# Ordering a two-layer hybrid backbone kernel by the scheduler's timing simulator

## The chip, the cores and the metric

The kernel runs on one core of a Trainium2 chip. The metric is the device time of one execution in microseconds, taken as the median over runs; before the change it is 2683.18 us over 3 runs (2682.48 to 2686.78).

## What is computed

The reference is a backbone of two layers (DEPTH = 2) over 256 latent tokens with a prefix of 256 context tokens, width 1024. Each layer has a token mixer with three branches and a SwiGLU feed-forward network, and layer norms after both. In layer 0 latent and context tokens both go through; layer 1, the last, gives only the latent tokens.

```python
def mixer_sublayer(...):
    (hq_l, hff_l, hfb_l, hi_l, hg_l, aq_l, ak_l, av_l, mz_l, mx_l, mdt_l, gt_l) = jnp.split(h_lat @ w_in, IN_SPLITS, axis=-1)
    ...
    y = g_hg * (o_hg @ w_br_hg) + g_at * (o_at @ w_br_at) + g_mb * (o_mb @ w_br_mb)
    return y @ w_out
```

Branch `hg` is HGRN2, a gated linear recurrence in both directions with 8 heads; branch `at` is grouped-query attention with 8 query and 2 key heads; branch `mb` is the Mamba-2 state-space scan (SSD) in both directions, 32 heads in 4 groups. The input projection has 14912 columns, the feed-forward network 2816 hidden units. All data are float32.

## The kernel before

Activations lie with channels on the 128 partitions and tokens along the free axis: 512 columns (context, then latent) in layer 0, mostly 256 in layer 1. Every large product is made as three matmuls in a reduced float32 type, from a high and a low half of each factor (`mm3`): high by high, high by low, low by high.

**Weights.** The class `Weights` streams each weight in tiles of 128 by 1024. `_load` (L115) starts the transfer on SyncE's queue into one of 4 buffers (`wraw`); `_split` makes the high half on ScalarE (`wh`, L125) and the low half on VectorE (`wl`, L126), 3 buffers each. `take` keeps the loads 4 tiles and the splits 2 tiles ahead of the unit of matmuls that reads them. These matmuls write the PSUM tiles `g`, of which there are 3. All matmuls are recorded under L204, transposes under L208, ScalarE's operations under L190, most of VectorE's under L193, L196, L200 and L201.

**Order of the work.** The program is written as generators. `Weave` steps through two of them together: a main one with projections (the `g` matmuls), and a side one with a scan or an attention whose operations are small. So the order in which the instructions are written down already interleaves the two. Per layer the stages are: the state-space scan's four groups (SSD), then the HGRN2 heads, the gates, attention, the branch projections, the output projection, and the feed-forward network.

**The order on each engine** is not this written order. When the `TileContext` closes, a list scheduler plays the program on a model of the chip. Whenever the model has an engine free, the scheduler gives it, of the instructions whose inputs are there, the one that comes first in the written order; a tile's buffer is given out in the same way. The resulting order per engine is then fixed in the program: on the chip each engine goes through its queue in that order, and an instruction that waits holds back those behind it. `issue_after` (at the transposes of `ssd_tok` and the activations of `silus`) adds edges that pin some instructions behind others.

**The SSD stage**, to which the prediction's steps go: `ssd_dt` computes decays and writes them to the DRAM tile `sd`. For each head, `ssd_scan` then loads two broadcasts of it on GpSimd's queue (L810 and L831 of the code below), builds the decay matrix and multiplies:

```python
for i in range(2):
    h = 8 * g + 2 * pr + i
    ab = self.b(name="ab")
    nc.gpsimd.dma_start(out=ab.rearrange("p (d t) -> p d t", d=2),
                        in_=bass.AP(sd.tensor, sd.offset + h * ts, [[0, P], [32 * ts, 2], [1, T]]))
    D, M = self.b(name="D"), self.b(name="M")
    ...
    e = self.a(name="ce")
    ...
yp = self.ps("y")
```

From `ab`, VectorE makes `D` and ScalarE parts of `M` (an exponential); ScalarE takes the exponential of `D`, VectorE adds parts of it into `M` and multiplies `M` by `cb` (L193). Then the matmuls `y<-M,xt` and `y<-ce,state` are made for the two heads in turn, which lie in two halves of the array's columns. `ab`, `D` and `M` come from a pool of 10 buffers (`n_b`), four of which hold `xt`, `cb` and `state` of the group. GpSimd's queue also carries other transfers: `sd` (L663, L666), the gates that layer 1 writes out early (`gd<-gate`, L1104), `ym`, `ys` and their reloads.

The line that is changed opens the `TileContext`; it is in `kernel`:

## Time and profile before

| | |
|---|---|
| median of 3 runs | 2683.18 us |
| the profiled execution's own time | 2682.9 us |
| its span, first to last instruction | 2681.0 us |
| mean granted TensorE clock | 0.991 of full |
| TensorE matmuls (PE) busy | 2597.5 us, 97%, 18660 matmuls |
| weight loads (PEld) busy | 2139.5 us, 80% |
| VectorE (DVE) busy | 1782.2 us, 66% |
| ScalarE (ACT) busy | 1233.2 us, 46% |
| GpSimd (POOL) busy | 193.0 us, 7% |
| DMA | 374.41 MB, mean 140 GB/s |

The profile is of one execution. Its own time is 1.9 us more than its span and 0.3 us under the median. A matmul's record overlaps the next one's, so that busy time of TensorE is time in which at least one is under way. "Idle before" an instruction is the time in which its engine had nothing, with what ended it after the arrow. SP is SyncE; a "q" after an engine marks what its sequencer issues, DMAs for instance. Names stand as out<-in.

### The profile page before, as it was taken

What the parts mean: (1) busy time and instruction counts of PE and PEld (TensorE: products, weight loads), DVE (VectorE), ACT (ScalarE), POOL (GpSimd) and SP (SyncE); (2) the same over time, 40 slices, a digit from 0 to 9 for tenths busy, and PEclk for the clock granted to TensorE, in tenths of its full rate; (3) what the DMA queues carried; (4) which work ended last, traced back from release to release, by engine and by line L of the source; (5) the groups of instructions that cost most, each with busy time, mean ns of one, the idle gap of its engine ahead of it and who ended that gap; (6) DMA issues with size and microseconds to landing.
All of it is one profiled execution on the core that took longest, in us unless ns stands there. A gap on an engine that the chain in (4) does not pass through costs nothing. (4 is left out here: it accounts for less than half of the span.)

```text
span 2681.0 us, 46307 instructions
## 1 busy us (share of the span) xinstructions
PE 2597.5 (97%) x18660; PEld 2139.5 (80%) x18660; DVE 1782.2 (66%) x3708; ACT 1233.2 (46%) x2030; POOL 193.0 (7%) x320
## 2 busy tenths in 40 slices
PE   7999989999999999999999999899999999999999
PEld 4767667788888897777888878677878898888998
DVE  5887776756565575457533358887877777857555
ACT  3655554632333324545432226565654334465543
POOL 0111010000000001010000000111110011111000
PEclk9999999999999999999999999899999999999999
DMA  7566555544444444352333323455763353446553
GB/s 248 147 178 178 147 163 157 150 120 116 118 142 134 123 138 154 94 194 70 102 95 102 95 79 99 132 161 161 222 185 108 98 144 109 140 122 201 166 183 109
DMA packets 298952, 374.41 MB, mean 140 GB/s; under 512 B 16433, under 2 KB 251985, under 8 KB 298737
## 3 DMA queue, kind: packets, MB, share of 16 engines
q1 hardware_dynamic: 271568, 284.21, 35.2%
q0 software_dynamic: 25728, 84.61, 11.1%
q8 instruction: 147, 2.41, 0.4%
q10 hardware_dynamic: 1440, 2.62, 0.3%
q14 instruction: 69, 0.56, 0.1%
HBM read 355.27 MB, written 16.12 MB: 139 GB/s over the span
## 5 line engine op out<-in xcount | busy, mean ns | idle before, releaser
L126 DVE TENSOR_TENSOR wl<-wraw,wh 128x1024 fp32r<-128x1024 f32 (+1 forms) x450 | 544.0, 1211 | 417.1 <-ACT wh L125 408.6
L125 ACT ACTIVATE wh<-wraw 128x1024 fp32r<-128x1024 f32 (+1 forms) x450 | 470.9, 1048 | 699.1 <-PE g L204 509.9
L204 PE MATMUL g<-hh,wh 128*128 128x512 f32 (+2 forms) x2032 | 731.8, 362 | 4.8 <-ACT hh L190 2.2
L204 PE MATMUL g<-hh,wl 128*128 128x512 f32 (+2 forms) x2032 | 723.0, 357 | 5.3 <-DVE wl L126 5.3
L204 PE MATMUL g<-hl,wh 128*128 128x512 f32 (+2 forms) x2032 | 724.6, 357 | 0.0
L204 PEld LDWEIGHTS g<-hh,wh 128*128 128x128 f32 (+1 forms) x2032 | 386.5, 191 | 75.9 <-issue 15.5
L204 PEld LDWEIGHTS g<-hh,wl 128*128 128x128 f32 (+1 forms) x2032 | 386.8, 191 | 68.7 <-issue 9.5
L204 PEld LDWEIGHTS g<-hl,wh 128*128 128x128 f32 (+1 forms) x2032 | 387.4, 191 | 61.8 <-issue 12.9
L204 PE MATMUL g<-oh,wh 128*128 128x512 f32 (+1 forms) x864 | 300.9, 350 | 2.4 <-DVE gl L193 1.3
L204 PE MATMUL g<-ol,wh 128*128 128x512 f32 (+1 forms) x864 | 295.3, 342 | 0.2 <-DVE ol L196 0.2
L204 PE MATMUL g<-oh,wl 128*128 128x512 f32 (+1 forms) x864 | 292.8, 340 | 0.5 <-DVE wl L126 0.5
L204 PE MATMUL g<-wh,hh 128*128 128x256 f32 x768 | 220.7, 287 | 0.0
L204 PE MATMUL g<-wh,hl 128*128 128x256 f32 x768 | 219.2, 285 | 0.0
L204 PE MATMUL g<-wl,hh 128*128 128x256 f32 x768 | 218.1, 284 | 0.0
L204 PEld LDWEIGHTS g<-oh,wh 128*128 128x128 f32 x864 | 163.7, 190 | 29.6 <-issue 7.9
L204 PEld LDWEIGHTS g<-ol,wh 128*128 128x128 f32 x864 | 164.3, 190 | 22.7 <-issue 6.3
L204 PEld LDWEIGHTS g<-oh,wl 128*128 128x128 f32 x864 | 164.0, 190 | 20.2 <-issue 2.7
L204 PEld LDWEIGHTS g<-wh,hh 128*128 128x128 f32 x768 | 147.1, 192 | 3.1 <-issue 2.6
L204 PEld LDWEIGHTS g<-wh,hl 128*128 128x128 f32 x768 | 147.2, 192 | 2.2 <-issue 1.9
L204 PEld LDWEIGHTS g<-wl,hh 128*128 128x128 f32 x768 | 147.2, 192 | 0.5 <-issue 0.4
L196 DVE SCALAR_TENSOR_TENSOR u<-craw,vec,u 128x508 f32<-128x508 f32 (+3 forms) x192 | 130.6, 721 | 8.6 <-ACT u L190 7.6
L196 DVE SCALAR_TENSOR_TENSOR D<-ab,tk,neg 128x128 f32<-128x128 f32 x384 | 110.2, 346 | 22.3 <-DMA ab<-sd 22.1
(303 smaller groups left out, 3577.7 us busy)
## 6 DMA issues: line engine op xcount, KB each, us to landing
wraw<-in_w_in SPq DMA_DIRECT2D x216, 512.0 KB, 4.1
wraw<-in_w_mod SPq DMA_DIRECT2D x96, 512.0 KB, 4.1
wraw<-in_w_ffn_in SPq DMA_DIRECT2D x88, 512.0 KB, 3.5
ab<-sd POOLq DMA_DIRECT2D x64, 512.0 KB, 6.8
wraw<-in_w_ffn_out SPq DMA_DIRECT2D x40, 512.0 KB, 3.4
ce<-sd POOLq DMA_DIRECT2D x64, 256.0 KB, 7.6
wraw<-in_w_br_mb SPq DMA_DIRECT2D x32, 512.0 KB, 3.4
wraw<-in_w_in SPq DMA_DIRECT2D x34, 256.0 KB, 3.6
```

The costliest lines, as they stand in the source:

```text
L125: self.nc.scalar.activation(hi[:, 0:n], t[:, 0:n], AF.Copy)
L126: self.nc.vector.tensor_tensor(out=lo[:, 0:n], in0=t[:, 0:n], in1=hi[:, 0:n], op=ALU.subtract)
L196: return self.nc.vector.scalar_tensor_tensor(out=out, in0=a, scalar=s, in1=b, op0=op0, op1=op1)
L204: return self.nc.tensor.matmul(out, l, r, start=start, stop=stop)
```

## The change

The `TileContext` is made with `schedule_with_timeline_sim=True`. The list scheduler then plays the program on the library's timeline simulator, in which queues and DMA transfers take time, in place of the plainer model. No line that computes is touched: the same instructions with the same sizes are scheduled, in an order that can differ on every engine and every DMA queue, and with buffers given out in another order.

```diff
-    with tile.TileContext(nc) as tc:
+    with tile.TileContext(nc, schedule_with_timeline_sim=True) as tc:
         with ExitStack() as ctx:
             Net(tc, io, ctx).run(out)
```

## Rows read from the trace of the kernel before

**Rows 1.** The page, part 1: span, and busy time of TensorE's matmuls.

```profile
span 2681.0 us, 46307 instructions
...
PE 2597.5 (97%) x18660; PEld 2139.5 (80%) x18660; DVE 1782.2 (66%) x3708; ACT 1233.2 (46%) x2030; POOL 193.0 (7%) x320
```

**Rows 2.** Busy time by stretch: us; busy (count) per engine; clock; DMA share; GB/s.

```profile
0.00:36.10 36.10, 17.29 (x256) 9.56 (x256) 10.04 (x33) 7.93 (x12) 3.01 (x9) 1.00 0.92 324
...
1340.00:1541.00 201.00, 201.00 (x889) 166.48 (x888) 72.66 (x79) 57.19 (x70) 0.00 (x0) 1.00 0.32 97
...
1676.00:2010.00 334.00, 307.06 (x1878) 247.69 (x1877) 266.93 (x528) 202.41 (x359) 52.12 (x76) 0.96 0.60 173
```

**Rows 3.** Waits of TensorE: engine, line, releaser, us in total, times, longest.

```profile
PE y L204 <- DVE M L193: 25.1, 13, 6.5
...
PE g L204 <- DVE wl L126: 5.8, 5, 2.3
```

**Rows 4.** Busy time by stretch: those in which the granted clock is half.

```profile
389.20:396.00 6.80, 3.83 (x9) 2.52 (x10) 6.01 (x14) 3.17 (x6) 0.00 (x0) 0.50 0.26 91
...
1727.20:1737.50 10.30, 7.48 (x29) 5.32 (x31) 5.81 (x13) 3.20 (x8) 2.14 (x3) 0.50 0.56 158
1812.60:1816.00 3.40, 3.40 (x14) 2.71 (x13) 3.23 (x6) 2.16 (x4) 2.13 (x3) 0.50 0.46 134
1979.80:1983.20 3.40, 3.40 (x16) 2.07 (x13) 1.15 (x4) 1.12 (x2) 0.71 (x1) 0.50 0.68 209
...
sum 47.80, PE 40.33 PEld 28.93 DVE 35.09 ACT 28.04 POOL 7.30; mean PE 5.04 PEld 3.62 DVE 4.39 ACT 3.50 POOL 0.91
```

**Rows 5.** Waits of all engines: two on landings, one on TensorE's release.

```profile
ACT wh L125 <- PE g L204: 509.9, 244, 7.5
...
ACT M L190 <- DMA ab<-sd: 51.3, 24, 5.6
...
DVE D L196 <- DMA ab<-sd: 22.1, 14, 4.9
```

**Rows 6.** Instructions in order of time, 380 to 393 us: start, length, engine, line.

```profile
380.30 0.71 POOL L810 DMA_DIRECT2D ab<-sd  x1 [11.07 <-PE g L204]
...
382.77 1.06 ACT L190 ACTIVATE D<-D 128x1024 f32<-128x1024 f32 x1 [1.47 <-DVE D L196]
...
383.25 1.22 DVE L126 TENSOR_TENSOR wl<-wraw,wh 128x1024 fp32r<-128x1024 f32 x1
...
389.41 0.61 DVE L196 SCALAR_TENSOR_TENSOR D<-ab,tk,neg 128x128 f32<-128x128 f32 x2 [4.95 <-DMA ab<-sd]
389.47 1.28 ACT L190 ACTIVATE M<-ab,tk 128x128 f32<-128x128 f32 x4 [5.64 <-DMA ab<-sd]
...
392.17 0.66 PE L204 MATMUL y<-M,xt 128*64 128x256 f32 x1 [6.50 <-DVE M L193]
```

**Rows 7.** Instructions in order of time, GpSimd's queue, 1677 to 1740 us.

```profile
1686.99 0.72 POOL L810 DMA_DIRECT2D ab<-sd  x1
1715.29 0.59 POOL L1104 DMA_DIRECT2D gd<-gate  x1 [27.57 <-ACT gate L190]
1719.64 0.56 POOL L1104 DMA_DIRECT2D gd<-gate  x1 [3.77 <-ACT gate L190]
...
1720.90 1.43 POOL L810 DMA_DIRECT2D ab<-sd  x2
```

**Rows 8.** The page, part 6: one group of DMA issues, us to landing.

```profile
ab<-sd POOLq DMA_DIRECT2D x64, 512.0 KB, 6.8
```

**Rows 9.** Groups by line, ScalarE: weight splits and table loads; busy us, mean ns.

```profile
L125 ACT ACTIVATE wh<-wraw 128x1024 fp32r<-128x1024 f32 (+1 forms) x450 | 470.9, 1048 | 699.1 <-PE g L204 509.9 <-issue 120.5 <-DMA wraw<-in_w_in 27.4
L190 ACT ACT_TABLE_LOAD x51 | 65.4, 1283 | 3.5 <-DVE s L196 1.9 <-PEq L1572 0.7
```

**Rows 10.** The chain that ended last: start, length, what.

```profile
1746.67 1.91 PE y L204 x14
...
2336.46 1.73 PE PV L204 x8
```

## The prediction

> **What bounds the kernel now.** The first view is the busy time of the engines: TensorE's matmuls cover 2597.5 of 2681.0 us, so it is without any work for 83.5 us [rows 1]. No other engine is above 66%. The next view is busy time by stretch. From 1340 to 1541 us TensorE is busy for all of 201.00 us: there the order of the instructions can give nothing. The first 36.1 us have 17.29 us of matmuls under a DMA share of 0.92 and 324 GB/s: weights of the modulation are awaited. The state-space scan of layer 1, from 1676 to 2010 us, has 307.06 of 334.00 us, so 26.9 us are idle, and its mean clock is 0.96 [rows 2]. Third come TensorE's own waits. The largest is that of the scan's `y` matmuls for `M` from VectorE, 25.1 us in 13 places [rows 3]. Fourth, the stretches at half the granted clock (1.2 in place of 2.4 GHz), 47.8 us in eight pieces; each begins behind idle time of TensorE, and a matmul there takes twice its time, so that they lose up to 23.9 us more [rows 4].
>
> How much room is that in all? The rows say 83.5 us idle plus 23.9 us of clock, 107 us or 4%, of which the start's 18.8 us (36.10 - 17.29) is a matter of transfers. The Trainium skill (Perfetto Trace Analysis, Identifying the Most-Contended Engine) holds matmul busy time for a poor measure and takes the busy share of the weight loads: at 80% that would leave 541 us, several times as much. Here the measurement decides: in the stretch without a gap the weight loads fill 166.48 of 201.00 us, 83%, so that 80% is nearly full [rows 1, 2].
>
> **What the change can move.** The same instructions run in another order. Rows show where the present order suits the transfers badly. At 380.30 us the load of `ab` is issued, and it is used at 389.41 us. VectorE's next instruction in the queue, a `D` that reads it, waits 4.95 us, and ScalarE's, an `M`, 5.64 us. Behind them in both in-order queues stand the next weight splits; TensorE ends its last `g` and waits 6.50 us at the `y` that needs this `M` [rows 6]. The median from issue to landing is 6.8 us, over 64 loads [rows 8]. In total ScalarE waits 51.3 us and VectorE 22.1 us for such landings at the head of their queues [rows 5]. A scheduler that gives a transfer time sees that the data are not there and puts the splits, and with them `g` matmuls, first. That is the mechanism I forecast.
>
> **The sum**, against the profiled execution's 2682.9 us (the median of the runs is 0.3 us above it):
>
> 1. Waits of `y` for `M`: 25.1 us [rows 3]. At best all go, at worst none. I take half, -12.5 us: the landing is hidden behind other work, but the `g` matmuls that can be drawn forward are few (three weight buffers, three PSUM tiles), and a late `ab` still delays `y`. What is late next is the buffer of `ab`, which comes free only when a head's work is done.
> 2. The clock behind these waits: the pieces at 389, 1727, 1812 and 1979 us last 6.8 + 10.3 + 3.4 + 3.4 = 23.9 us and lose up to half, 12.0 us [rows 4]. Half of that goes with the waits, -6.0 us; bounds 0 and -12.0.
> 3. GpSimd's queue: after the `ab` at 1686.99 us it waits 27.57 and 3.77 us for two gates to write out, and only then issues the next two `ab`, at 1720.90 us [rows 7]. Moved ahead, these loads would end the hunger for work there. The `y` waits are counted above; what is added are waits of `g` for `wl`, 5.8 us in five places [rows 3], of which I take 2.5. Bounds 0 and -5.8.
> 4. The start. All its loads must land in any order, and they take 0.92 of the DMA time of 36.1 us [rows 2]; a better order can gain 0.08 x 36.1 = 2.9 us, a worse one as much. I take 0.
> 5. SyncE's weight loads and the splits behind them: cost nothing, since ScalarE waits 509.9 us in 244 places for TensorE to free `wh` [rows 5]; the splits are early. If that cover went in one place, a split of 1.05 us would be on the path [rows 9].
> 6. Table loads of ScalarE: 51 of 1.283 us [rows 9]. Another mix of activations needs more or fewer, and one in front of a split that TensorE awaits is on the path. Bounds: ten fewer or ten more on the path, 12.8 us either way. I take three more, +3.8 us, because the scan's exponentials will stand among other work more often.
> 7. Order on TensorE. `y` matmuls of two heads share the array: 14 records in 1.91 us, 136 ns each, where undivided ones of the same width take 216 ns (8 in 1.73 us) [rows 10]. If `g` were put among them, 640 records would lose at most 80 ns each, 51 us. I take 0: they become ready together, and next to each other in the written order they stay together.
>
> Sum: 2682.9 - 12.5 - 6.0 - 2.5 + 3.8 = 2665.7 us, and with the median's 0.3 us 2666 us, 0.64% faster. With every wait of `y`, its clock and term 3 gone and no new table load it is 2683.2 - 25.1 - 12.0 = 2646 us, less up to 5.8; I set the low end at 2644.
>
> The Trainium skill (DMA: Bandwidth & Descriptors, Anatomy of one DMA) fits a GpSimd DMA as 2.0 us plus its bytes over 436 GB/s; an estimate by it for 512 KB is 3.2 us. The trace disagrees, with 6.8 us in the median [rows 8]. If the simulator reckons as that fit does, it speaks against the change: the order would hide only half of each landing, terms 1 and 2 would halve, and the time would be 2675 us.
>
> **The rivals.**
>
> *Nothing to be measured* (2683 us, within 5.4 us; 0.2% is about what a measurement of this kernel can tell from no change). For it: 83.5 us of idle time in 2681, and long stretches with none [rows 1, 2]; the order also goes by the written order, which is kept, so that engines swap only neighbours. What is moved off VectorE's and ScalarE's heads may have cost TensorE nothing: they wait 73.4 us for landings [rows 5], and TensorE only 25.1 us for `M`. That the order comes out as it was belongs here. Against it: 46307 instructions, and hundreds of choices that hang on times. Chance 0.21.
>
> *Slower, by GpSimd's queue.* It is in order and carries the loads of `ab` and `ce` together with writes of gates, which wait for a projection. Where a write gets in front of a head's load, the scan starves: that is what happens at 1715 us, and around it TensorE loses the 2.6 us of a `y` wait and about as much of a `wl` wait (term 3's 2.5) and half of the 10.3 us at half clock: 10.3 us in all [rows 4, 7]. With transfers that take time, a load has to wait longer in the model for its buffer, while the write's data are there when TensorE says so; so writes can get in front more often. Layer 1 has four groups with a gate chunk each; if it happens in two more, the time is 2683.2 + 20.6 = 2704 us. It decides from the point at which one more write stands in front than now without any `y` wait won. For it speaks that it is there once already; against it, that a simulator which knows the landing can also issue loads early. Chance 0.29, in which I put other new waits of the kind, table loads (term 6) and divided `y` groups (term 7) as well.
>
> **How the numbers follow.** Forecast, with its mechanism at any size over 0.2%: 0.50, its own range 2644 to 2677. No change: 0.21. Slower: 0.29. So faster 0.50, same 0.21, slower 0.29. The predicted time is that of the likeliest case, 2666 us. The range runs from 2644 to 2704 us: the low end is the whole of terms 1 to 3, the high end two more starved groups; beyond these I leave 0.05 below and 0.15 above (a starved group in all four, or divided `y` groups).
>
> **What would show it.** Right: in the changed kernel's trace ScalarE's `M` and VectorE's `D` wait well under 73.4 us for `ab`, `y` waits for `M` around 12 us, the half-clock pieces of the scans are fewer, and no `gd` write with a long wait stands between two `ab` loads of a group. Wrong: the landing waits are gone while TensorE's busy time and idle time stay (the rival without change); or idle time moves to other waits of `g` and `y`, with new pieces at half clock; or the table loads rise well over 51. The prediction also fails if the gain comes from the first 36 us, or from stretches that have no gap now.

## The result, and the profile after

The change makes the kernel slower: 2828.4 us (2826.0 to 2831.0, 4 runs) against 2685.0 us (2682.5 to 2687.5, 4 runs) of the kernel before on the same chip, a ratio of 1.0538 with a 95% interval of 1.0523 to 1.0554. The forecast was 2666 us, its range ended at 2704 us.

Of the experiments below, `list_pe2`, `list_all4`, `pe2_pool_plain` and `second_layer_pe2` were run 4 times and `first_layer_pe2` 10 times, the others once; runs of the kernel before lie between 2677.0 and 2690.1 us over all chips used.

First the page of the changed kernel: span and busy time.

```profile
span 2829.1 us, 46316 instructions
...
PE 2659.8 (94%) x18660; PEld 2166.4 (77%) x18660; DVE 1778.6 (63%) x3708; ACT 1226.6 (43%) x2023; POOL 192.8 (7%) x320
```

Against [rows 1] TensorE's idle time goes from 83.5 to 2829.1 - 2659.8 = 169.3 us, +85.8 us, and its busy time grows by 62.3 us over the same 18660 matmuls. VectorE, ScalarE and GpSimd work as long as before to within 7 us. So the other engines do no more work than before; TensorE stands bare twice as long, and its matmuls take longer.

A part of that is the clock. These are stretches of the changed kernel with half the granted clock, 24 in all without the end of the program: length, busy time of TensorE, its weight loads, VectorE, ScalarE, GpSimd, then clock, DMA share and GB/s.

```profile
1052.60:1059.40 6.80, 5.70 (x13) 3.16 (x14) 3.02 (x12) 2.50 (x6) 0.00 (x0) 0.50 0.25 77
...
1772.80:1789.80 17.00, 5.31 (x23) 4.18 (x22) 11.97 (x21) 5.16 (x10) 3.04 (x5) 0.50 0.41 102
...
2612.40:2626.10 13.70, 6.74 (x27) 5.87 (x27) 11.29 (x34) 8.69 (x19) 0.00 (x0) 0.50 0.16 50
...
sum 146.90, PE 105.01 PEld 79.97 DVE 109.50 ACT 64.21 POOL 19.37; mean PE 4.38 PEld 3.33 DVE 4.56 ACT 2.68 POOL 0.81
```

Before, there were eight such pieces with 47.8 us [rows 4]. What the slower clock lengthens is busy time: TensorE is busy in these stretches for 105.01 us, in those of before for 40.33 us, and half of the difference, at most 32.3 us, goes to the clock. With the 85.8 us of idle time that is 118 of the 148.1 us by which the span grew. The other 30 us are busy time too, and were followed only in part: the records of `mod` cover 82.2 us in place of 70.0, those of `y` (`M,xt` and `ce,state`) 129.6 us in place of 117.8, slower clock and overlap with other records included. Why stays open.

Where does it happen? Both kernels make the same 450 weight splits on VectorE (L126), and the starts of the 130th, 170th and so on cut both into comparable stages. Six stages of the kernel before, in the columns above: the first layer's scan (splits 0 to 60, counted from 0 in the order run), its HGRN2 heads (60 to 130), its attention (130 to 170), its output and feed-forward work (170 to 220), the boundary with the second layer's scan (220 to 300), the second layer's attention (340 to 390).

```profile
36.10:505.20 469.10, 453.33 (x2580) 330.52 (x2581) 369.89 (x716) 261.17 (x431) 47.05 (x67) 0.99 0.57 162
505.20:1010.50 505.30, 501.46 (x5146) 427.50 (x5146) 311.77 (x702) 169.92 (x242) 14.67 (x27) 1.00 0.43 127
1010.50:1312.50 302.00, 301.80 (x1596) 235.86 (x1595) 175.76 (x393) 149.23 (x265) 25.81 (x48) 1.00 0.40 128
1312.50:1584.00 271.50, 271.50 (x1199) 224.90 (x1198) 107.74 (x126) 75.57 (x92) 0.00 (x0) 1.00 0.31 94
1584.00:2039.20 455.20, 427.85 (x2628) 345.07 (x2627) 357.65 (x721) 271.95 (x490) 56.47 (x84) 0.97 0.53 152
...
2235.50:2490.50 255.00, 243.23 (x1963) 215.17 (x1962) 190.05 (x513) 136.31 (x246) 38.92 (x72) 0.97 0.47 146
```

And the same stages of the changed kernel:

```profile
35.60:535.50 499.90, 476.59 (x2615) 339.19 (x2614) 369.13 (x715) 264.29 (x433) 46.97 (x67) 0.97 0.54 155
535.50:1036.40 500.90, 500.12 (x5100) 427.25 (x5099) 306.52 (x687) 166.54 (x237) 14.63 (x27) 1.00 0.42 125
1036.40:1375.20 338.80, 319.10 (x1607) 243.77 (x1607) 179.09 (x411) 149.45 (x266) 26.11 (x48) 0.97 0.36 114
1375.20:1646.80 271.60, 271.60 (x1199) 224.87 (x1199) 107.77 (x127) 75.57 (x92) 0.00 (x0) 1.00 0.31 94
1646.80:2141.30 494.50, 441.21 (x2611) 349.23 (x2610) 356.84 (x720) 268.72 (x488) 56.45 (x84) 0.94 0.49 140
...
2342.80:2633.50 290.70, 249.37 (x1954) 219.43 (x1952) 193.80 (x518) 132.74 (x243) 38.58 (x72) 0.94 0.41 128
```

The feed-forward stage is equal to 0.1 us. The first attention loses 36.8 us, and it had not a microsecond of idle time before (301.80 of 302.00). The two attentions and the second scan lose 36.8 + 39.3 + 35.7 = 111.8 us, the first layer's scan another 30.8 (499.9 against 469.1 us). These are stages in which a chain of small operations runs beside the projections. The HGRN2 heads have such a chain too, and their stage is 4.4 us shorter; but the stages are cut at weight splits, and a piece of that chain has slid behind the cut (`oT` at 1045 us, below). The attention's chain of scores and transposes (`S`, `p`, `PT`, `PV`) contains no transfer.

TensorE's waits in the changed kernel (releaser, us in total, times, longest):

```profile
PE y L204 <- DVE M L193: 15.8, 7, 4.6
PE spread L204 <- DVE diag L193: 15.5, 5, 4.7
PE oT L208 <- DVE sq L196: 10.4, 5, 3.9
PE g L204 <- DVE hl L193: 9.3, 3, 3.6
PE dtT L208 <- DVE dy L193: 8.9, 1, 8.9
PE PT L208 <- DVE s L196: 7.2, 3, 3.3
...
PE g L204 <- DVE wl L126: 6.3, 4, 3.2
```

The wait that the forecast wanted gone, `y` for `M`, did shrink, from 25.1 us [rows 3] to 15.8. In its place stand many small ones, most of them at a matmul of a chain of small operations, the rest at projections that need its results (`hl`) or a split (`wl`). From the waits of the other engines:

```profile
ACT wh L125 <- PE g L204: 576.1, 270, 6.3
...
ACT M L190 <- DMA ab<-sd: 74.3, 25, 6.1
...
ACT oh L190 <- PE oT L208: 49.8, 14, 8.2
...
DVE D L196 <- DMA ab<-sd: 38.6, 20, 4.3
...
DVE ce L193 <- DMA ce<-sd: 9.9, 8, 2.1
```

and of the kernel before, for the second load of each head:

```profile
DVE ce L193 <- DMA ce<-sd: 23.5, 17, 3.6
```

The waits for landings of `ab` at the head of the two queues, 73.4 us before [rows 5], are now 112.9 us. With those for `ce` the sum goes from 96.9 to 122.8 us. A scheduler that knows of transfers has made them more, not fewer.

One place shows the pattern: instructions in order of time in the changed kernel's first attention (start, length, engine, line, what; in brackets the idle time before).

```profile
1041.11 1.13 DVE L196 SCALAR_TENSOR_TENSOR sq<-o,s,g 128x128 f32<-128x128 f32 x4
...
1044.77 0.39 PE L204 MATMUL g<-oh,wl 128*128 128x512 f32 x1
1045.00 0.27 PE L208 MATMUL oT<-ident,sq 128*128 128x128 f32 x1
...
1046.07 0.69 ACT L190 ACTIVATE oh<-oT,vec 128x512 fp32r<-128x512 f32 x1 [8.16 <-PE oT L208]
...
1049.37 1.06 ACT L125 ACTIVATE wh<-wraw 128x1024 fp32r<-128x1024 f32 x1 [2.12 <-PE g L204]
1050.44 1.28 ACT L190 ACT_TABLE_LOAD   x1
1051.74 0.56 ACT L190 ACTIVATE p<-S,s 128x256 f32<-128x256 f32 x1
...
1053.32 0.45 PE L208 MATMUL PT<-ident,p 128*128 128x128 f32 x1 [3.31 <-DVE s L196]
```

`sq` belongs to the last HGRN2 head. All four of its pieces are written by 1042.24 us, but TensorE's queue holds twelve more `g` ahead of the first `oT`, which starts at 1045.00, 2.8 us later. ScalarE stood idle for 8.16 us before `oh`. Then a weight split and a table load stand ahead of `p`, and between the last `g` and `PT` TensorE's queue holds no other matmul: TensorE is bare for 3.31 us, and the clock has gone to half at 1052.6 us, the first piece above. The projections were spent early, in front of the chain, and are missing when the chain is all there is.

### The profile page after: what moved, and what is told of

It reads as the page before. It is cut to its first block, busy times and chain, and to the rows that moved or that the text cites. A ratio compares the mean times of both kernels' runs of the same rounds, so it can differ in the third digit from the quotient of the medians.

```text
span 2829.1 us, 46316 instructions
## 1 busy us (share of the span) xinstructions
PE 2659.8 (94%) x18660; PEld 2166.4 (77%) x18660; DVE 1778.6 (63%) x3708; ACT 1226.6 (43%) x2023; POOL 192.8 (7%) x320
## 3 DMA queue, kind: packets, MB, share of 16 engines
q0 software_dynamic: 25728, 84.61, 10.4%
## 5 line engine op out<-in xcount | busy, mean ns | idle before, releaser
L126 DVE TENSOR_TENSOR wl<-wraw,wh 128x1024 fp32r<-128x1024 f32 (+1 forms) x450 | 544.5, 1210 | 500.5 <-ACT wh L125 489.7
L125 ACT ACTIVATE wh<-wraw 128x1024 fp32r<-128x1024 f32 (+1 forms) x450 | 471.5, 1049 | 768.4 <-PE g L204 576.1
L204 PEld LDWEIGHTS g<-hl,wh 128*128 128x128 f32 (+1 forms) x2032 | 390.5, 192 | 69.5 <-issue 10.4
L196 DVE SCALAR_TENSOR_TENSOR D<-ab,tk,neg 128x128 f32<-128x128 f32 x384 | 107.1, 344 | 39.3 <-DMA ab<-sd 38.6
```

Of the source, the lines that this page charges most:

```text
L125: self.nc.scalar.activation(hi[:, 0:n], t[:, 0:n], AF.Copy)
L126: self.nc.vector.tensor_tensor(out=lo[:, 0:n], in0=t[:, 0:n], in1=hi[:, 0:n], op=ALU.subtract)
L196: return self.nc.vector.scalar_tensor_tensor(out=out, in0=a, scalar=s, in1=b, op0=op0, op1=op1)
L204: return self.nc.tensor.matmul(out, l, r, start=start, stop=stop)
```

## The experiments

The kernels below are built twice in one program where orders are held: first with one model, to read its orders, then with the other, with an ordering edge (no semaphore) from each instruction of a held engine to the one ahead of it in the order read.

```diff
-    with tile.TileContext(nc) as tc:
-        with ExitStack() as ctx:
-            Net(tc, io, ctx).run(out)
...
+        with tile.TileContext(nc, schedule_with_timeline_sim=timeline) as tc:
+            with ExitStack() as ctx:
+                Net(tc, io, ctx).run(out)
+            pin(tc, nc, pins)
...
+        first, _ = build(PIN_FROM, {})
+        pins = orders(first)
...
+    nc, arrays = build(TIMELINE, pins)
```

**Is it the order at all?** The timing simulator, all five engines held to the plain model's orders.

> Scheduled on the timing simulator, but with the order of every engine and queue tied to that of the kernel before; only the giving out of buffers is left to the simulator. If the order makes the 143 us, as every theory here says: 2685 us, within 5. If the buffers given out matter: over 2700 us.

2679.4 us, with 2683.1 us of the kernel before on that chip. The loss is in the orders of the engines. Buffers given out differently cost nothing here: in this kernel, as built, 1033 of 4294 tiles lie at another address than before. SyncE's order is no part of it, since its instructions come in the same order in the kernel before, in the change and with every length of list below.

**Which engine's order?** Three mixtures: TensorE's order alone from the plain model, TensorE's order alone from the simulator, and VectorE's and ScalarE's from the plain model.

> Timing simulator, with TensorE's order alone tied to that of the kernel before. Theory T (TensorE's order does it: its g matmuls stand too far ahead of the scan's and attention's own matmuls, whose chain is then late and left bare): near before, 2685 to 2715 us. Theory V (the order of VectorE and ScalarE, splits against scan work): still over 2800 us. Theory P (GpSimd's queue, my rival): still over 2800 us.

> Plain model, with TensorE's order alone tied to that of the changed kernel; the other engines are ordered around it. Theory T: 2790 to 2830 us. Theories V and P: near before, under 2715 us.

> Timing simulator, with the orders of ScalarE and VectorE tied to those of the kernel before, TensorE free. Theory T: still slow, over 2780 us. Theory V: near before, 2685 to 2715 us. Theory P: over 2800 us.

They measured 2798.9, 2903.9 and 2896.3 us: 4.3, 8.2 and 7.9% over before, the last two worse than the change itself. None of the theories T, V and P meets all three: T wanted 2685 to 2715 us from the first, V and P under 2715 us from the second. Putting back TensorE's order alone, or VectorE's and ScalarE's, does not undo the loss, and the simulator's order on TensorE alone costs more than all of its orders together; the orders of one model fit each other. In the last two mixtures the splits come late. TensorE with the simulator's order above the plain model's splits:

```profile
PE g L204 <- DVE wl L126: 39.7, 8, 11.8
```

and the simulator's TensorE above the plain model's VectorE and ScalarE:

```profile
PE g L204 <- DVE wl L126: 41.7, 37, 3.7
...
PE g L204 <- ACT wh L125: 17.7, 12, 3.6
```

Before, that wait was 5.8 us [rows 3]. Mixing orders cannot separate the cause, and a new theory was needed. The simulator keeps, for each engine, a list of instructions that are handed over and not finished; the library's table gives it 35 places for TensorE and 12 for the others. Theory Q: an instruction gets its place in the order when it enters that list, many matmuls before it runs, when the side chain's next matmul isn't ready yet. The scheduler then fills the list with the ready `g` matmuls, and the chain's matmul stands behind them.

**How long a list?** The change itself, with the table altered only while the order is made:

```diff
+QDEPTH = {'PE': 2}
...
+    t = hw_specs.get_hw_spec("TRN2").ENG_ISSUE_QUEUE_DEPTH
+    kept = dict(t)
+    for e in t:
+        n = str(e).split(".")[-1]
+        if n in d:
+            t[e] = d[n]
...
+    table, kept = depths(QDEPTH)
...
+    nc, arrays = build(TIMELINE, pins)
+    table.update(kept)
```

> The edit: the timing simulator sets the orders as in the change, but while it does so, the list of instructions that it lets stand handed over and unfinished on TensorE is cut from 35 to 2 (the other engines keep 12). Theory Q (the scheduler has to choose a matmul when the simulator's list takes it, some 35 matmuls before it runs, so a matmul of the scan or of attention that becomes ready later stands behind that many of the projections): most of the loss goes, 2660 to 2710 us, TensorE idle near before's 83.5 us instead of 169.3. Theory L (the landings and durations in the simulator give the bad order, however long the list is): 2800 to 2850 us as in the change. Theory O (the lists of VectorE and ScalarE, 12 each, are what is too long): 2780 to 2840 us.

> The edit: as the change, with the simulator's lists of VectorE, ScalarE, GpSimd and SyncE cut from 12 to 2 and TensorE's left at 35. Theory Q (TensorE's list): 2800 to 2840 us, no more than 1% from the change. Theory O (the other engines' lists): 2660 to 2720 us. Theory L (landings, durations): 2800 to 2850 us.

> The edit: as the change, with the simulator's lists of all engines cut to 4 instructions. Theory Q: 2650 to 2710 us; if the simulator's landings are worth anything once the lists are short, this is below before, at 2655 to 2680. Theory O: 2650 to 2710 too. Theory L: 2800 to 2850 us.

> The edit: as the change, with TensorE's list in the simulator cut from 35 to 16 (the other engines keep 12). Theory Q: a loss that grows with the list, so between the run with 2 and the change, 2700 to 2770 us. Theories O and L: 2800 to 2850 us.

> The edit: as the change, with TensorE's list in the simulator lengthened from 35 to 70 (the others keep 12). Theory Q: the loss grows with the list, 2900 to 3000 us, with still more idle time of TensorE ahead of the matmuls of the scan and of attention. Rival S (35 is already long enough that nothing more is committed early, because the buffers of the weights end the run-ahead): 2810 to 2850 us.

The table gives the result by length of TensorE's list, with the length of three stages between the same weight splits, the mean granted clock, and the lead of the projections in the first attention. That lead is counted in the order on TensorE: for each matmul of the chain (`qT`, `S`, `PT`, `PV`, as far as they are among the first 11000 instructions written) the number of `g` matmuls ahead of it, less the number written ahead of it, and the mean of these.

| kernel | us | clock | first attention, us | second scan, us | second attention, us | lead of `g` |
|---|---|---|---|---|---|---|
| before (plain model) | 2684 | 0.991 | 302.0 | 455.2 | 255.0 | 18 |
| list of 2 | 2705.1 | 0.989 | 306.8 | 466.1 | 266.2 | 22 |
| list of 16 | 2736.1 | 0.984 | 314.5 | 476.5 | 282.8 | 40 |
| list of 35 (the change) | 2828.4 | 0.973 | 338.8 | 494.5 | 290.7 | 54 |
| list of 70 | 2943.7 | 0.958 | 353.0 | 507.3 | 314.1 | 59 |

With a list of 2 the ratio to before is 1.0073 (1.0052 to 1.0093): 123.3 of the 143.4 us that the change lost hang on one number in a table, and the loss grows with that number as theory Q expected. Rival S, that 35 is long enough already, falls with the list of 70. TensorE's idle time is then 2699.2 - 2594.6 = 104.6 us, not quite the 83.5 us of before. With all lists at 4 the ratio is 1.0076 (1.0057 to 1.0096); that short lists would bring the time below before did not come true. With TensorE's list at 35 and the others at 2, 2818.3 us: theory O falls. That the list's length decides, and that the lead in the first attention grows with it, is shown. That a matmul's place is settled when it enters the list is argued from this, and the mean lead doesn't measure the loss everywhere. Counted in the same way for the second layer's attention it is already 57 before, then 56, 60, 64 and 66 down the table, while that stage loses 11.2, 27.8, 35.7 and 59.1 us. With a list of 2, the waits are these, TensorE's first:

```profile
PE y L204 <- DVE M L193: 12.6, 14, 2.1
...
PE PT L208 <- DVE p L200: 4.7, 4, 1.6
PE oT L208 <- DVE sq L196: 4.4, 2, 3.8
...
PE spread L204 <- DVE diag L193: 1.4, 1, 1.4
```

```profile
ACT M L190 <- DMA ab<-sd: 73.3, 30, 6.4
...
DVE D L196 <- DMA ab<-sd: 31.1, 20, 3.7
...
ACT oh L190 <- PE oT L208: 23.5, 11, 4.5
```

The waits of `oT` and `spread` are less than half of the change's 10.4 and 15.5 us, and ScalarE waits 23.5 us for `oT` in place of 49.8. The landing waits of `ab`, however, are still 104.4 us, while 123 us of the time are gone: they were not what the change lost most by.

**Are the landings what is left?** The list of 2, and a start of GpSimd's transfers that is 3 us later in the simulator, so that consumers of `ab` are placed later.

```diff
+START = {'Pool': 3000}
...
+    t = hw_specs.get_hw_spec("TRN2").DGE_DMA_DELAY
+    old = dict(t)
...
+        for e in t:
+            t[e] += d.get(str(e).split(".")[-1], 0)
```

> The edit: TensorE's list in the simulator at 2 as in the run list_pe2 (2705 us), and while it schedules, every transfer that GpSimd issues starts 3 us later than the simulator's own constant says. Theory U (the simulator takes the scan's loads for quicker than the measured 6.4 us, so it still places their consumers too early, and that is what is left of the loss): the waits for the landing of ab fall from 104 us to under 60, and the time to 2670 to 2695. Theory N (the landings do not set what is left): the landing waits may fall, the time does not: 2700 to 2790 us.

2747.8 us. The landing waits go from 104.4 to 11.8 us, as theory U wanted, and the kernel becomes 43 us slower:

```profile
PE y L204 <- DVE M L193: 55.3, 27, 5.2
```

```profile
ACT M L190 <- DMA ab<-sd: 11.8, 8, 2.5
```

VectorE has no wait for `ab` left. What the two engines no longer wait at the head of their queues, TensorE waits at `y`: 55.3 in place of 12.6 us, about what the kernel loses. The second layer's scan alone takes 499.8 in place of 466.1 us. This is the cleanest answer to the forecast's mechanism: hiding the landings of `ab` by placing their consumers later brings nothing. It does not show that these waits are free in every order: GpSimd's order, next, takes them down together with the time. The Trainium skill's fit of a GpSimd DMA (DMA: Bandwidth & Descriptors, Anatomy of one DMA) gives an estimate of 3.2 us for these loads; the runs disagree, with medians of 5.9 to 7.1 us.

**GpSimd's queue**, the slower rival of the prediction: the change with GpSimd held to the order of before, first with TensorE's list at 35, then at 2.

> The edit: as the change, but GpSimd's queue (64 ab loads, the loads and writes of gd and its arithmetic) is held to the order that it has in the kernel before; TensorE, VectorE, ScalarE and SyncE stay with the timing simulator and its lists of 35 and 12. Theory Q (TensorE's list of 35): 2800 to 2860 us, the landing waits change little. Theory P (the prediction's slower case: GpSimd writes gate rows ahead of the scan's ab loads): 2690 to 2730 us, and the waits for the landing of ab fall from 112.9 us to before's 73.4 or under.

> The edit: TensorE's list in the simulator at 2, as in list_pe2 (2705 us), and GpSimd's queue held to the order of the kernel before. With the list at 35 that order of GpSimd was worth 24 us (2828 to 2804). Theory G (what list_pe2 still loses is GpSimd's order): 2675 to 2692 us, and the landing waits fall from 104 us to under 75. Theory R (it is not): 2698 to 2720 us, whatever the landing waits do.

With 35 it is 2804.2 us, 24 us better than the change, though from one run. The landing waits, which theory Q expected to change little, are 61.6 us, less than before the change:

```profile
ACT M L190 <- DMA ab<-sd: 43.7, 22, 6.2
DVE D L196 <- DMA ab<-sd: 17.9, 13, 3.0
```

So that queue's order is worth about a sixth of the loss, and theory P as the main cause falls. The 24 us lie in the two scans, 485.7 in place of 499.9 us in the first layer and 484.0 in place of 494.5 us in the second; the attentions stay as they are in the change. With 2 it is 2699.6 us, ratio 1.0057 (1.0042 to 1.0072) against 1.0073 of list_pe2; the two intervals overlap, although the landing waits fall from 104.4 to 76.6 us. The rest of 0.6 to 0.7% isn't GpSimd's order.

**Where the rest is, and a kernel that beats both.** The plain model for the whole program, with the orders of the list of 2 held on all engines, once for the first 11000 instructions written and once for those behind. The seam lies near the end of the first layer's attention: 27 of its 176 matmuls `S`, `PT` and `PV` are written behind it.

> The edit: the plain model as in the kernel before, with all five engines held, for the instructions written up to the end of the first layer's attention, to the orders of the run list_pe2; what is written later the plain model orders for itself. In list_pe2 those stages ended 3 to 8 us earlier than before, and the loss came in the second layer. If the gain of the first layer stays by itself: 2675 to 2682 us, 0.1 to 0.3% under before. If what stood at the seam moves back into the second layer: 2684 to 2700 us.

> The edit: the plain model, with all five engines held to the orders of list_pe2 for the instructions written behind the first layer's attention, the mirror image of first_layer_pe2. If the two halves add up: list_pe2 is 21 us over before and its first part gains about 11, so the rest costs about 32, and this kernel takes 2708 to 2722 us. If the loss came from what the first part hands over to the second: 2680 to 2695 us.

The first measured 2672.4 us (10 runs), ratio 0.9965 (0.9954 to 0.9976): faster than both kernels. The second measured 2708.9 us, ratio 1.0094 (1.0076 to 1.0112). Stages of the first one, in the columns of the stretches above; the first line is the first layer's scan, which takes 469.1 us in the kernel before:

```profile
34.30:496.70 462.40, 452.93 (x2566) 330.69 (x2565) 367.22 (x714) 258.69 (x428) 46.93 (x67) 0.99 0.58 166
...
998.30:1300.50 302.20, 301.42 (x1599) 237.90 (x1598) 176.24 (x393) 148.47 (x265) 26.00 (x48) 1.00 0.40 128
...
1572.10:2027.90 455.80, 427.82 (x2628) 346.68 (x2627) 357.73 (x721) 271.98 (x490) 56.29 (x84) 0.97 0.53 152
```

The gain is made up to the end of the first layer's HGRN2 stage (1.8 us at the start, 6.7 us in the scan, 3.7 us in HGRN2) and stays; the stages behind are those of before. So the simulator, once its list is short, orders the part ahead of the seam better than the plain model, by 0.35% of the whole time, and the part behind it worse, by 0.9%. Why it is worse there stays open: GpSimd's order and what the first part hands over are excluded as its main part, and taking the landing waits away made it worse.

## Why the prediction was wrong

The step that failed is the mechanism itself: "A scheduler that gives a transfer time sees that the data are not there and puts the splits, and with them `g` matmuls, first." It does put them first, but also where no transfer is near, as in the first attention, and too many of them. The forecast took the change for the plain model with transfers added. What came with the timing simulator, a list of 35 places on TensorE, wasn't considered, and the length of TensorE's list is the cause of 123 of the 143 us lost (2828.4 against 2705.1 and 2685.0 us). With it fell the sentence of the first rival that "engines swap only neighbours": the mean lead of the projections over the chain in the first attention went from 18 to 54 matmuls.

By its terms:

1. Waits of `y` for `M`: forecast -12.5 us, measured 25.1 to 15.8, -9.3 us; with the list of 2, -12.5 us. That the size is near is luck, since the reason is wrong: the landing waits of `ab` that were to vanish grew by 39.5 us, and where they all but vanish (11.8 us) `y` waits 55.3 us. "What is late next" was sought at `ab`'s buffer; it was `oT`, `spread`, `dtT`, `PT` and `hl`.
2. The clock: forecast -6.0 us; half-clock time went from 47.8 to 146.9 us, at most +32.3 us by its busy part. The forecast's own price was too high: it halved the whole of the pieces, idle time included. Of the 47.8 us TensorE is busy for 40.33, so at most 20.2 us and not 23.9 are lost to the clock, and for the four pieces of this term, busy for 18.1 us, at most 9.1 and not 12.0.
3. GpSimd's queue: forecast -2.5 us; in the change its order costs about 24 us, but this is a sixth of the loss. That the slower rival's price, 20.6 us, is near is luck. It stood for gate writes in front of the loads of two more groups of the second layer, and no more groups have them: in the kernel before two gate writes already stand ahead of loads of `ab` in all four groups, where the forecast saw one. For the second group before:

```profile
1794.33 0.56 POOL L1104 DMA_DIRECT2D gd<-gate  x1 [40.37 <-ACT gate L190]
1796.37 0.56 POOL L1104 DMA_DIRECT2D gd<-gate  x1 [1.47 <-ACT gate L190]
1796.92 0.72 POOL L810 DMA_DIRECT2D ab<-sd  x1
```

   What differs is the first group: one of its eight `ab` is issued ahead of the gates before [rows 7], none in the change. And 14 of the 24 us lie in the first layer's scan, in which no gate is written.
4. The start: 0. The first split starts at 35.6 us (36.1 before [rows 2]): right.
5. SyncE and the splits' cover: ScalarE waits 576.1 us for TensorE to free `wh`, more than before [rows 5]. Right in the change; in the last two mixtures of orders this cover was gone, and `g` waited 39.7 and 41.7 us for `wl`.
6. Table loads: forecast three more; there are 44 in place of 51 [rows 9], 56.5 us in place of 65.4. Wrong in sign; what that is worth on the path isn't shown.
7. Divided `y` groups: forecast 0. They do get divided: the 640 `y` records stand on TensorE in 76 unbroken rows in place of 62, 8 of them with 14 records in place of 16. The time that `y` records cover grew by 11.8 us, slower clock included; no run tests this by itself.

The forecast also took room for gain as the measure: 107 us could be won. What could be lost it sized for GpSimd's queue, table loads and divided `y` groups alone, and not for stages that had no gap, although the first attention, 301.80 of 302.00 us busy beside a chain of small operations, is full only as long as projections are left to fill it. Here it lost 36.8 us. One of the forecast's own signs of being wrong came: idle time moved to other waits, with new pieces at half clock. The Trainium skill's measure (Perfetto Trace Analysis, Identifying the Most-Contended Engine), the busy share of the weight loads, went from 80% to 77%: it agrees with the sign, but doesn't show where.

## What to carry to other kernels

A list scheduler that runs far ahead spends the filler work in front of the latency-bound chain (that it does so by committing a matmul early is the likely reading, not a shown one); ask of any scheduler at what moment it chooses, not only what it knows, and try its run-ahead as a parameter before judging its model. An in-order engine that waits for a landing at the head of its queue is no measure of what can be gained: look whether the bottleneck engine waits behind it, and expect that hiding the landing by placing its consumer later can move the wait there, as it did here. When two schedules differ, don't expect one engine's order to carry the difference: orders of one schedule belong together, and a mixture can be worse than either, while whole stages can be exchanged at a seam.

## What the runs showed of the hardware that was not expected

Gaps are paid for again in clock. As the list grows from 2 to 70, the mean clock falls from 0.989 to 0.958. In the change each of the 24 stretches at half clock begins in or just behind bare time of TensorE, and TensorE is busy in them for 105.01 of 146.90 us, so that short bare times cost up to 52.5 us more in the matmuls behind them. The loads of `ab` land in a median of 5.9 to 7.1 us in every order tried, though the spans differ by 270 us, and the median doesn't go with the time (5.9 us at 2804 us, 6.8 before, 6.4 at 2944): their time hardly depends on the order, who waits for it does.
